# A two-block transformer kernel: the second feed-forward's pairs computed with seven half-size products, and another PSUM bank for one of them

## The chip, the cores and the metric

The kernel runs as one program on one core of a Trainium2 chip. The metric is the device time of one execution in microseconds (us). Before the change the median of three runs is 1746.8 us (1745.65 to 1747.08). The engines are named as in the profile: PE is TensorE (matmuls), PEld its weight loads, DVE VectorE, ACT ScalarE, POOL GpSimd, SP the engine that issues most DMAs.

## The reference

Two transformer blocks run one after the other over 512 tokens with 1024 channels, in float32. Each ends in a gated feed-forward of 2816 hidden channels, and only these two feed-forwards are touched:

```python
D_FF = ((8 * D_MODEL + 3 * 256 - 1) // (3 * 256)) * 256        # 2816
# first block
u = rms_norm(h, norm_ffn_g[l])
g, up = jnp.split(u @ w_gate_up[l], 2, axis=-1)
h = h + (jax.nn.silu(g) * up) @ w_down[l]
# second block
h = rmsnorm(x, g_ffn_pre[l])
gu = h @ w_ffn_in[l]
f = (jax.nn.silu(gu[..., :D_FF_2]) * gu[..., D_FF_2:]) @ w_ffn_out[l]
x = x + rmsnorm(f, g_ffn_post[l])
```

The rest of the first block is a block-sparse attention, a chunked mLSTM and their gated merge; the rest of the second is three attentions and their gated merge.

## The kernel before, in words

**Layout.** Activations lie with channels on the 128 partitions and tokens along the free dimension. Every float32 operand is split into a high part `hi` (a rounding copy on ACT) and a low part `lo` (the difference, on DVE), and each product is three matmuls: hi·hi, hi·lo, lo·hi. All of them are issued through `mm` (L231), so the trace shows one line for nearly all PE work. Weights come from HBM in chunks (`raw`, two buffers) and are split by `emit_split` (L331: ACT at L358, DVE at L359) into `whi` and `wlo`, six buffers each (`NSPLIT`). `next_half` (L364) decides how far ahead of the matmuls the splitting runs; in "deep" mode it fills all six buffers.

**A feed-forward** (`ffn`, L1261) has 22 pairs. A pair is one tile of 128 gate channels and one of 128 up channels. They are done in three parts of 8, 7 and 7 pairs; after each part the down projection adds that part's contribution to all 8 output tiles. A normal pair is 2 tiles x 8 k-tiles x 3 = 48 matmuls of 512 columns (`fm_tile`, L394). Gate and up tiles accumulate in the three PSUM banks `pd`; DVE multiplies them by the row norm `R`, ACT applies silu, DVE multiplies gate and up, and the result is split again into hi and lo (tiles `Ba`/`Bb` and `Ca`/`Cb`).

**Seven products.** `SEVEN = {"f1": 1}` (L131): in the first feed-forward all pairs but the first are computed as a 2 x 2 block product with seven half-size products in place of eight. The blocks are gate/up, the two halves of the 1024 input channels, and the two halves of the 512 tokens. Each product is 4 k-tiles x 3 = 12 matmuls of 256 columns, so a pair has 84 of them. It needs sums of weight blocks and sums of activation blocks. The weight sums `s1` and `s3` are made by accumulating DMAs on the POOL queue (L306, L307: the transfer issued by SP at L304 and L305 is added to), two more on DVE (L322). The activation sums `t1` to `t4` are made once per feed-forward in four steps by `seven_prep` (L412): step k makes four 256-column differences in the tile `M4` (one buffer) on DVE (L428 to L431), a rounding copy of all four on ACT and their lo part on DVE (both through `split_to`, L537 and L538). A product reads k-tile k of them, so the fourth step is needed by the last three matmuls of the first product with a `t`.

`seven` (L438) orders the products of a pair as head ("11"), mid ("t3", "t2", "21", "t1") and tail ("22", "t4"); a pair's tail is issued after the head of the next one. There are three accumulators: `g0` (11, then 21), `g1` (t2, t1, 22, begun from a copy of `g0` made by ACT at L459, "the seeding copy") and `c0` (t3, t4). `g0` and `c0` are the two halves of one `ps` bank; the `g1` of even and odd pairs are the two halves of a bank `po` that is set to zero once (L435). PE runs the products in exactly this order (`strict`, L221).

**The second feed-forward** (`f2`) has no seven products. Its first three pairs are done in two passes over token halves (`fm_halves`, L491), so that the first half of the tokens starts while the second half's norm is still being made: POOL adds up squares (L597), a matmul with ones sums over channels, POOL takes the power -0.5 (L603, `rc_q`), PE broadcasts it by four transposes (L615) and ACT copies it into `R`. The first four of those six half-pass weight blocks, and likewise the first four of the last six down blocks, are split into tiles of their own, tags `Yh`, `Yl`, `Y` and `G` (`self.place`, L255).

The instruction order on each engine is made by the framework's scheduler when the program is built; engines run their queues in that order. Pools give a buffer only after its last reader.

Of the kernel before, what the change touches and what calls it, by code (L numbers as in the profile page):

```python
# [8 lines left out]
F32 = mybir.dt.float32  # L9
F32R = mybir.dt.float32r  # L10
# [7 lines left out]
P = 128  # L18
# [109 lines left out]

SEVEN = {"f1": 1}  # L131
HEAD, MID, TAIL = ("11",), ("3", "2", "12", "1"), ("4", "22")
NWARM = 40
MOBA_C = 0
# [2 lines left out]
NSPLIT = 6  # L137
# [9 lines left out]
class Build:  # L147
# [216 lines left out]
    def next_half(self, expect, ahead=None):  # L364
        i = self.wi
        name, ci, j, L, kt, w = self.halves[i]
        assert name == expect, (name, expect)
        if ahead is None and self.deep:
            cost = lambda k: 0 if k in self.place else 1 if self.halves[k][0].endswith("_7") else CUT
            n, ahead = cost(i), 0  # L370
            while i + ahead + 1 < len(self.halves) and n + cost(i + ahead + 1) <= NSPLIT:
                ahead += 1
                n += cost(i + ahead)
        elif ahead is None:
            ahead = 0 if expect in TOKEN_MAJOR else 1
        while self.next_split <= i + ahead and self.next_split < len(self.halves):
            self.emit_split()
        self.wi += 1
        return self.split.pop(i)
# [32 lines left out]
    def seven_prep(self, u, th, tl, src, g):  # L412


        nc = self.nc
        lo, hi = slice(0, 256), slice(256, 512)
        x = {}
        for i, (d, w) in enumerate(((0, lo), (4, lo), (4, hi))):
            x[("11", "21", "22")[i]] = [lambda k, p=p, d=d, w=w: u[p][:, k + d, w] for p in range(2)]
        for i in range(4):  # L420
            x["t%d" % (i + 1)] = [lambda k, p=p, i=i: p(k)[:, i, :] for p in (th, tl)]

        def step(k):
            a, b = self.tmp(), self.tmp()
            self.act(a, src(k), AF.Copy, scale=g(k))
            self.act(b, src(k + 4), AF.Copy, scale=g(k + 4))
            t = self.t("M4", [P, 4, 256])
            nc.vector.tensor_sub(t[:, 0, :], a[:, lo], a[:, hi])  # L428
            nc.vector.scalar_tensor_tensor(t[:, 1, :], t[:, 0, :], -1.0, b[:, hi], op0=ALU.mult, op1=ALU.subtract)
            nc.vector.tensor_sub(t[:, 2, :], b[:, hi], a[:, hi])  # L430
            nc.vector.scalar_tensor_tensor(t[:, 3, :], t[:, 1, :], -1.0, b[:, lo], op0=ALU.mult, op1=ALU.subtract)  # L431
            self.split_to(th(k), tl(k), t)

        self.seeded = self.bk_o()
        nc.tensor.matmul(self.seeded, self.zb, self.zb[:, None, :].to_broadcast([P, 4, P]), start=True, stop=True)  # L435
        return x, [lambda k=k: step(k) for k in range(4)]

    def seven(self, name, x, pairs, evac):  # L438

        nc = self.nc

        def product(ps, b, start=False):
            hi, lo = x[b]
            kw = dict(skip_group_check=True)
            for k, (wh, wl) in enumerate(self.next_half(name)):
                self.mm(ps, wh, hi(k), start=start and k == 0, stop=False, **kw)
                self.mm(ps, wh, lo(k), start=False, stop=False, **kw)
                self.mm(ps, wl, hi(k), start=False, stop=k == 3, **kw)  # L450

        def head(q):
            b = self.bk_s()
            q["g0"], q["c0"] = b[:, 0:256], b[:, 256:512]
            q["g1"] = self.seeded[:, 256 * (q["j"] % 2):256 * (q["j"] % 2) + 256]
            product(q["g0"], "11", True)

        def mid(q):
            nc.scalar.copy(q["g1"], q["g0"])  # L459
            q["u2"], q["u4"] = self.t("s7", [P, 256], F32, bufs=2), self.t("s7b", [P, 256], F32, bufs=1)  # L460
            product(q["c0"], "t3")
            product(q["g1"], "t2")
            nc.scalar.copy(q["u2"], q["g1"])
            product(q["g0"], "21")
            product(q["g1"], "t1")
            nc.scalar.copy(q["u4"], q["g1"])
            q["lin"] = self.tmp()
            nc.vector.tensor_add(q["lin"][:, 256:512], q["u4"], q["c0"])

        def tail(q):  # L470
            product(q["g1"], "22")
            gate = evac[0](q["g0"], q["g1"])
            product(q["c0"], "t4")
            nc.vector.tensor_add(q["lin"][:, 0:256], q["u2"], q["c0"])
            evac[1](q["j"], gate, q["lin"])
            self.done_tile(lambda: None)

        self.strict = "start"
        last = None
        for j in pairs:  # L480
            q = dict(j=j)
            head(q)
            if last is not None:
                tail(last)
            mid(q)
            last = q
        if last is not None:
            tail(last)
        self.strict = None

    def fm_halves(self, name, n, rhs_hi, rhs_lo, evac, between=None):  # L491
# [766 lines left out]
        yield from self.pipeline(units, [s0, s1, s2, s2b, s3])  # L1258


    def ffn(self, name, u, st, down_evac, part_hook=None, halves=None, x7=None):  # L1261
        nc = self.nc
        uh, ul = u
        rh, rl = self.acc_k(uh), self.acc_k(ul)
        f0 = 0
        for p, n in enumerate(FF_PARTS):
            ah, al = self.pair_tiles("Ba", "Bb"), self.pair_tiles("Ca", "Cb")
            sil = {}

            full = slice(0, S)  # L1270

            def ev_g(ps, j, w=full):
                a = self.tmp()[:, w]
                nc.vector.tensor_mul(a, ps, st["R"][:, w])
                self.last_silu = self.act(a, a, AF.Silu).ins
                sil[j, w.start] = a

            def ev_u(ps, j, w=full):
                b = self.tmp()[:, w]
                nc.vector.tensor_mul(b, ps, st["R"][:, w])  # L1280
                a = sil.pop((j, w.start))
                nc.vector.tensor_mul(a, a, b)
                self.split_to(ah(j)[:, w], al(j)[:, w], a)

            j0 = 0
            if halves is not None and p == 0:
                j0 = NUP // 2
                self.fm_halves(name + "_up", NUP, rh, rl, lambda ps, i, w: (ev_u if i % 2 else ev_g)(ps, i // 2, w),
                               halves)
                self.strict = None  # L1290

            def ev_7g(g0, g1):
                a = self.tmp()
                nc.vector.tensor_mul(a[:, 0:256], g0, st["R"][:, 0:256])
                nc.vector.tensor_mul(a[:, 256:512], g1, st["R"][:, 256:512])
                self.last_silu = self.act(a, a, AF.Silu).ins
                return a

            def ev_7(j, a, lin):
                nc.vector.tensor_mul(lin, lin, st["R"])  # L1300
                nc.vector.scalar_tensor_tensor(a, lin, -1.0, a, op0=ALU.mult, op1=ALU.mult)
                self.split_to(ah(j), al(j), a)

            j7 = n if name not in SEVEN else min(max(SEVEN[name] - f0, j0), n)
            for j in range(j0, j7):
                self.fm(name + "_up", rh, rl, lambda ps, j=j: ev_g(ps, j))
                self.fm(name + "_up", rh, rl, lambda ps, j=j: ev_u(ps, j))
            self.seven(name + "_7", x7, range(j7, n), (ev_7g, ev_7))
            f0 += n
            if part_hook is not None:  # L1310
                part_hook(p)
            k0 = KD - NDN if halves is not None and p == 2 else KD
            for k in range(k0):
                self.fm(name + "_dn", ah, al, lambda ps, k=k: down_evac(ps, k, p, full))
            if k0 < KD:
                self.fm_halves(name + "_dn", NDN, ah, al, lambda ps, i, w: down_evac(ps, k0 + i, p, w))


    def block1(self):
        nc = self.nc  # L1320
        x = self.x
        u = uh, ul = self.new_u()
# [7 lines left out]
        for k in range(KD):  # L1330
            i = k % 2
            self.sq_add(accs[i], x[:, k, :], k < 2, eng=nc.gpsimd if i == 0 else nc.vector)
        st, hooks = self.stat_hooks(accs, "a")
# [17 lines left out]
        q = lambda h: qt_[:, h, :]  # L1351
# [86 lines left out]
        u = uh, ul = self.new_u()  # L1438
        acc = self.t("A", [P, S], F32, bufs=2)

        def ev_wo(ps, k):
# [3 lines left out]

        th = [self.t(tag, [P, 2, 4, 256], F32R) for tag in ("Yh", "Yl")]
        tl = [self.t(tag, [P, 2, 4, 256], F32R) for tag in ("V8", "K8")]
        x7, steps = self.seven_prep(u, lambda k: th[k // 2][:, k % 2], lambda k: tl[k // 2][:, k % 2],
                                    lambda k: h[:, k, :], lambda k: self.vec("norm_ffn_g", k))
        for k in range(KD):  # L1450
            self.fm("wo", *mp["m"], lambda ps, k=k: ev_wo(ps, k))
# [47 lines left out]
    def block2(self, nx):  # L1499
        nc = self.nc  # L1500
# [4 lines left out]
        u = uh, ul = nx["u"]  # L1505
# [231 lines left out]
        def between():  # L1737
            self.hooks = list(hx[256])
# [27 lines left out]
                else:  # L1766
                    self.later = [[0, g] for g in hk + [e[1] for e in self.later] + fs]

        self.ffn("f2", u, st, ev_dn, None, between)

    def run(self):
        self.prologue()
# [80 lines left out]
```

## Time and profile before

| | |
|---|---|
| profiled execution, whole | 1746.25 us |
| its span (first to last instruction) | 1744.3 us |
| median of three runs | 1746.8 us |
| PE busy | 1717.9 us, 98% |
| DVE busy | 1128.6 us, 65% |
| ACT busy | 871.2 us, 50% |
| granted TensorE clock, mean | 0.994 of 2.4 GHz |

Busy times count overlapping instructions once. A matmul's recorded duration is longer than its distance to the next one, since matmuls are pipelined; what a matmul costs is read from start to start. In the rows below a time is the start of an instruction in us from the start of the span, followed by its duration; brackets hold the idle time ahead of it and what ended it.

### The profile page before, as it was taken

The numbers are of one execution on the slowest core, as the hardware profiler recorded it, in microseconds if no ns is written. First come the engines' busy times: TensorE is split into PE (matmuls) and PEld (weight loads), VectorE is DVE, ScalarE is ACT, GpSimd is POOL, SyncE is SP. The second block draws the span as 40 slices with busy tenths as digits, with TensorE's granted clock in tenths as the row PEclk, the third lists the DMA queues.
The fourth block names the chain that finished last, engine by engine and source line by source line (L and its number), as shares of the span: only waits on it lengthen the run. The fifth ranks groups of instructions, "written<-read, shape, count | busy, mean of one in ns | idle before, by whom it ended". The sixth has DMA issues, their size and how long they took to land.

```text
span 1744.3 us, 25883 instructions
## 1 busy us (share of the span) xinstructions
PE 1717.9 (98%) x9601; PEld 1446.7 (83%) x9601; DVE 1128.6 (65%) x2363; ACT 871.2 (50%) x1767; POOL 152.6 (9%) x203
## 2 busy tenths in 40 slices
PE   8999999998999999999999999999999999999997
PEld 8878788887998989988989776777789988888887
DVE  5887665667865857787499945666655743344454
ACT  5755655545543635574455567654545433332331
POOL 1400011000100101000000222200001400000001
PEclk9999999999999999999999999999999999999999
DMA  5433225343654746335224122333233233333331
GB/s 181 119 100 117 78 61 151 121 145 85 163 146 121 179 130 151 83 116 172 85 73 122 49 73 61 109 85 111 71 121 107 63 99 95 97 92 99 95 112 50
DMA packets 65661, 187.04 MB, mean 107 GB/s; under 512 B 7840, under 2 KB 10440, under 8 KB 65280
## 3 DMA queue, kind: packets, MB, share of 16 engines
q1 hardware_dynamic: 59456, 174.33, 32.7%
q0 software_dynamic: 6080, 11.08, 3.9%
q8 instruction: 75, 1.23, 0.3%
q14 instruction: 50, 0.41, 0.1%
HBM read 174.87 MB, written 6.84 MB: 104 GB/s over the span
## 4 chain that ended last, share of the span: by engine, by line
PE 95%; DVE 2%; ACT 2%; POOL 0%; DMA 0%; issue 0%; SPq 0%; DVEq 0%; ACTq 0%
PE pd L231 67%; PE ps L231 7%; PE po L231 5%; PE po L797 2%; PE pd L524 2%; PE pd L526 2%; PE pd L525 2%; PE ps L574 1%; PE ps L575 1%; PE ps L787 1%; PE po L1196 1%; PE ps L1162 0%; DVE ul L541 0%; PE ps L1167 0%; PE po L973 0%
## 5 line engine op out<-in xcount | busy, mean ns | idle before, releaser
L358 ACT CAST whi<-raw 128x512 fp32r<-128x512 f32 (+3 forms) x536 | 308.2, 582 | 498.9 <-PE pd L231 383.7
L359 DVE TENSOR_TENSOR wlo<-raw,whi 128x512 fp32r<-128x512 f32 (+3 forms) x536 | 346.7, 652 | 246.2 <-ACT whi L358 241.4
L231 PE MATMUL pd<-uh,whi 128*128 128x512 f32 (+1 forms) x1032 | 406.0, 394 | 0.0
L231 PE MATMUL pd<-uh,wlo 128*128 128x512 f32 (+1 forms) x1032 | 405.1, 393 | 0.0
L231 PE MATMUL pd<-ul,whi 128*128 128x512 f32 (+1 forms) x1032 | 404.0, 391 | 0.0
L231 PEld LDWEIGHTS pd<-uh,wlo 128*128 128x128 f32 x1032 | 194.0, 188 | 45.4 <-issue 3.3
L231 PEld LDWEIGHTS pd<-ul,whi 128*128 128x128 f32 x1032 | 193.8, 188 | 41.3 <-issue 1.7
L231 PEld LDWEIGHTS pd<-uh,whi 128*128 128x128 f32 x1032 | 194.0, 188 | 40.7 <-issue 2.2
L231 PE MATMUL pd<-Ba,whi 128*128 128x512 f32 (+1 forms) x240 | 91.4, 381 | 0.0
L231 PE MATMUL pd<-Ca,whi 128*128 128x512 f32 (+1 forms) x240 | 90.9, 379 | 0.0
L231 PE MATMUL pd<-Ba,wlo 128*128 128x512 f32 (+1 forms) x240 | 90.7, 378 | 0.0
L231 PE MATMUL pd<-Cb,whi 128*128 128x512 f32 (+1 forms) x210 | 79.7, 380 | 0.0
L231 PE MATMUL pd<-Bb,wlo 128*128 128x512 f32 (+1 forms) x210 | 79.7, 379 | 0.0
L231 PE MATMUL pd<-Bb,whi 128*128 128x512 f32 (+1 forms) x210 | 78.3, 380 | 0.7 <-ACT Bb L537 0.7
L231 PE MATMUL pd<-Yh,whi 128*128 128x512 f32 (+1 forms) x192 | 72.5, 383 | 0.9 <-DVE H L753 0.9
L231 PE MATMUL pd<-Yl,whi 128*128 128x512 f32 (+1 forms) x192 | 72.4, 377 | 0.0
L231 PE MATMUL pd<-Yh,wlo 128*128 128x512 f32 (+1 forms) x192 | 72.4, 377 | 0.0
L526 PE MATMUL pd<-whi,ul 128*128 128x260 f32 (+1 forms) x232 | 64.9, 286 | 1.5 <-DVE ul L541 1.4
L524 PE MATMUL pd<-whi,uh 128*128 128x260 f32 (+1 forms) x232 | 65.4, 286 | 0.8 <-ACT uh L180 0.8
L525 PE MATMUL pd<-wlo,uh 128*128 128x260 f32 (+1 forms) x232 | 65.2, 283 | 0.0
L231 PEld LDWEIGHTS pd<-Ba,whi 128*128 128x128 f32 x240 | 45.0, 188 | 9.7 <-DVE H L1460 0.9
L231 PEld LDWEIGHTS pd<-Ba,wlo 128*128 128x128 f32 x240 | 45.1, 188 | 9.2
(525 smaller groups left out, 3698.4 us busy)
## 6 DMA issues: line engine op xcount, KB each, us to landing
raw<-in_wts SPq DMA_DIRECT2D x218, 512.0 KB, 3.5
raw<-in_wts SPq DMA_DIRECT2D x32, 448.0 KB, 3.4
PT<-in_wts SPq DMA_DIRECT2D x42, 256.0 KB, 3.8
PT<-in_wts POOLq DMA_DIRECT2D x42, 256.0 KB, 5.0
P<-in_wts SPq DMA_DIRECT2D x21, 256.0 KB, 3.2
raw<-in_wts SPq DMA_DIRECT2D x8, 520.0 KB, 3.5
tabd<-tab SPq DMA_DIRECT2D x8, 320.0 KB, 5.7
H<-in_xT SPq DMA_DIRECT2D x8, 256.0 KB, 5.1
```

Source lines behind the costliest of these rows:

```text
L231: return self.pe(self.nc.tensor.matmul(*args, **kw))
L358: self.nc.scalar.copy(hi, r)
L359: self.nc.vector.tensor_sub(lo, r, hi.bitcast(F32))
L524: mm(pss[i][:, :w], xh[:, kk, sl], hi, start=(kk == 0), stop=False)
L525: mm(pss[i][:, :w], xh[:, kk, sl], lo, start=False, stop=False)
L526: mm(pss[i][:, :w], xl[:, kk, sl], hi, start=False, stop=(kk == 7))
L574: mm(out, q, khi, start=True, stop=False)
L575: mm(out, q, klo, start=False, stop=True)
L787: nc.tensor.transpose(ps[:, kt * P:(kt + 1) * P], Pt[:, kt * P:(kt + 1) * P], self.ident)
L797: nc.tensor.matmul(o[64 * hh:64 * hh + 64, qt * P:(qt + 1) * P], v[:, kt, h * 64:(h + 1) * 64], PTs[hh][:, kt * P:(kt + 1) * P], start=(kt ...
L1196: nc.tensor.matmul(o[c][64 * hh:64 * hh + 64, kt * P:], bv[:, kt, h * 64:(h + 1) * 64], us[hh]["a"][:, :N], start=False, stop=True, skip_g ...
```

## The change

1. `SEVEN = {"f1": 2, "f2": 5}`: in the first feed-forward the second pair becomes a normal pair, so 20 pairs in place of 21 are done with seven products; in the second feed-forward pairs 5 to 21, 17 of 22, are.
2. `c0` gets a bank of its own (one of the three `pd` banks) in place of the second half of `g0`'s bank, and the seeding copy is issued behind the previous pair's product "22", ahead of its "t4".
3. In the second feed-forward the sums `t1` to `t4` are made by `halves_done`, called when the two passes are issued; the four steps are issued behind the first and second tile of pair 3. Their hi parts lie in `Yh` and `Yl`, their lo parts in the tags `Y` and `G`. Deep mode is switched on there.
4. In deep mode the splitting no longer runs ahead into a block that has a place of its own, so the four last down blocks are split into `Yh`, `Yl`, `Y` and `G` only when the products that read the sums there have been issued.

```diff
-SEVEN = {"f1": 1}
+SEVEN = {"f1": 2, "f2": 5}
...
-            while i + ahead + 1 < len(self.halves) and n + cost(i + ahead + 1) <= NSPLIT:
+            while i + ahead + 1 < len(self.halves) and n + cost(i + ahead + 1) <= NSPLIT and \
+                    i + ahead + 1 not in self.place:
...
-            self.split_to(th(k), tl(k), t)
+            nc.scalar.copy(th(k)[0], t)
+            n = 4 // len(tl(k))
+            for i, d in enumerate(tl(k)):
+                w = slice(i * n, (i + 1) * n)
+                nc.vector.tensor_sub(d, t[:, w, :], th(k)[0][:, w, :].bitcast(F32))
...
         def head(q):
-            b = self.bk_s()
-            q["g0"], q["c0"] = b[:, 0:256], b[:, 256:512]
+            q["g0"], q["c0"] = self.bk_s()[:, 0:256], self.bk_d()[:, 0:256]
...
+        def seed(q):
+            nc.scalar.copy(q["g1"], q["g0"])
+
         def mid(q):
-            nc.scalar.copy(q["g1"], q["g0"])
...
-            product(q["c0"], "t3")
+            product(q["c0"], "t3", True)
...
-        def tail(q):
+        def tail(q, between):
             product(q["g1"], "22")
+            between()
             gate = evac[0](q["g0"], q["g1"])
...
-            if last is not None:
-                tail(last)
+            if last is None:
+                seed(q)
+            else:
+                tail(last, lambda: seed(q))
             mid(q)
...
+        def halves_done():
+            th = [self.t(tag, [P, 2, 4, 256], F32R) for tag in ("Yh", "Yl")]
+            tl = [self.quad(tag, F32R, [P, 2, 256]) for tag in ("Y", "G")]
+            x7, steps = self.seven_prep(u, lambda k: [th[k // 2][:, k % 2]], lambda k: tl[k // 2][2 * (k % 2):2 * (k % 2) + 2],
+                                        X, lambda k: self.vec("g_ffn_pre_2", k))
+            self.later += [[1 + k // 2, f] for k, f in enumerate(steps)]
+            self.deep = True
+            return x7
```

**ACT, first feed-forward, one pair's change to the next.** Before, the seeding copy (L459, `po<-ps`) stands behind the silu of the previous pair (L180):

```order
L466 COPY s7b_5156<-po_4055 128x256
L358 CAST whi_5246<-PT_4845 128x512
L358 CAST whi_5268<-raw_5131 128x512
L180 ACTIVATE tmp_5262<-tmp_5262 128x512
L459 COPY po_4055<-ps_5229 128x256
L358 CAST whi_5292<-T_5294 128x512
```

Now (L465) it stands ahead of that silu and of one more weight cast:

```order
L473 COPY s7b_4747<-po_4055 128x256
L358 CAST whi_4908<-PT_4551 128x512
L358 CAST whi_4939<-raw_4793 128x512
L465 COPY po_4055<-ps_4888 128x256
L358 CAST whi_4960<-T_4962 128x512
```

The copy has moved up by one ACT instruction, and on PE the product behind it ("t3") writes another bank.

**DVE, second feed-forward, behind the up tile of the fifth pair (pair 4).** `pd` is that tile; `M` is `M4`, `G` the lo part of the sums, `Yl` their hi part. Before:

```order
L1280 TENSOR_TENSOR tmp_15175<-pd_15150,R_13970 128x512
L359 TENSOR_TENSOR wlo_15225<-raw_15180,whi_15224 128x512
L1282 TENSOR_TENSOR tmp_15137<-tmp_15137,tmp_15175 128x512
L538 TENSOR_TENSOR Cb_14522<-tmp_15137,Bb_14520 128x512
L359 TENSOR_TENSOR wlo_15261<-raw_15218,whi_15260 128x512
```

Now:

```order
L1290 TENSOR_TENSOR tmp_15224<-pd_15199,R_13925 128x512
L1292 TENSOR_TENSOR tmp_15186<-tmp_15186,tmp_15224 128x512
L359 TENSOR_TENSOR wlo_15240<-raw_15151,whi_15239 128x512
L438 TENSOR_TENSOR G_14985<-M_3267_15123,Yl_14980 128x512
L438 TENSOR_TENSOR G_14986<-M_3267_15123,Yl_14980 128x512
L359 TENSOR_TENSOR wlo_15257<-T_15258,whi_15256 128x512
L548 TENSOR_TENSOR Cb_14477<-tmp_15186,Bb_14475 128x512
L430 TENSOR_TENSOR M_3270_15135<-tmp_15131 128x256
L432 TENSOR_TENSOR M_3270_15135<-tmp_15132,tmp_15131 128x256
L322 TENSOR_TENSOR T_15394<-T_15309,raw_15151 128x512
L431 SCALAR_TENSOR_TENSOR M_3270_15135<-M_3270_15135,tmp_15132 128x256
L433 SCALAR_TENSOR_TENSOR M_3270_15135<-M_3270_15135,tmp_15132 128x256
```

The lo part of the third step and the whole fourth step stand behind the evacuation of pair 4's up tile; the ACT cast of the fourth step and two more `L438` follow.

**POOL, second feed-forward, the end of the second token half's sum of squares.** `A` is the sum, `PT_15002` and the like the weight sums of pairs 5 and 6. Before:

```order
L597 TENSOR_TENSOR A_13969<-A_13969,PT_14664 128x256
L597 TENSOR_TENSOR A_13969<-A_13969,PT_14672 128x256
L597 TENSOR_TENSOR A_13969<-A_13969,PT_14680 128x256
L603 TENSOR_TENSOR rc_q_14859<-small_14857,mhalf_142 128x2
L603 TENSOR_TENSOR rc_z_17341<-small_17339,mhalf_142 128x2
```

Now:

```order
L607 TENSOR_TENSOR A_13924<-A_13924,PT_14627 128x256
L306 DMA PT_15002<-in_wts 128x512
L607 TENSOR_TENSOR A_13924<-A_13924,PT_14635 128x256
L307 DMA PT_15001<-in_wts 128x512
L306 DMA PT_15072<-in_wts 128x512
L307 DMA PT_15071<-in_wts 128x512
L613 TENSOR_TENSOR rc_q_14814<-small_14812,mhalf_142 128x2
```

Four accumulating DMAs have come ahead of `rc_q`, one of them ahead of the last addition. Each waits until the transfer that it adds to has landed, and that transfer until its buffer is free of the sums of squares.

## Rows read from the trace of the kernel before

**Rows 1.** The page: busy time by engine; shares of the chain that ended last.
```profile
PE 1717.9 (98%) x9601; PEld 1446.7 (83%) x9601; DVE 1128.6 (65%) x2363; ACT 871.2 (50%) x1767; POOL 152.6 (9%) x203
...
PE 95%; DVE 2%; ACT 2%; POOL 0%; DMA 0%; issue 0%; SPq 0%; DVEq 0%; ACTq 0%
```
**Rows 2.** Windows: five seven-product pairs (first feed-forward), three normal pairs (second).
```profile
core 0: us, PE busy (x) PEld busy (x) DVE busy (x) ACT busy (x) POOL busy (x), PEclk, DMA share, GB/s
444.76:495.87 51.11, 50.95 (x423) 49.93 (x421) 45.69 (x80) 31.64 (x61) 7.81 (x9) 1.00 0.74 184
...
1415.03:1448.39 33.36, 33.36 (x145) 27.03 (x144) 15.69 (x25) 11.22 (x19) 0.00 (x0) 1.00 0.30 95
```
**Rows 3.** Timeline of PE at one seeding copy: start, duration, line, operation.
```profile
465.24 0.28 PE L231 MATMUL ps<-K,whi 128*128 128x256 f32 x1
465.36 0.28 PE L231 MATMUL ps<-Yl,wlo 128*128 128x256 f32 x1
465.67 0.38 PE L231 MATMUL ps<-Yh,whi 128*128 128x256 f32 x1
465.89 0.28 PE L231 MATMUL ps<-V,whi 128*128 128x256 f32 x1
```
**Rows 4.** Waits of PEld for the seeding copy: us in total, times, longest.
```profile
PEld ps L231 <- ACT po L459: 7.5, 21, 1.1
```
**Rows 5.** Timeline of PE at the second part's first seven-product pair.
```profile
550.92 0.29 PE L231 MATMUL ps<-uh,wlo 128*128 128x256 f32 x1
552.06 0.39 PE L231 MATMUL ps<-Yh,whi 128*128 128x256 f32 x1 [0.86 <-ACT po L459]
```
**Rows 6.** Timeline of PE in the first feed-forward's first seven-product pair.
```profile
432.34 0.49 PE L231 MATMUL ps<-Yl,whi 128*128 128x256 f32 x1 [3.69 <-ACT Yl L537]
433.60 0.58 PE L231 MATMUL ps<-K,whi 128*128 128x256 f32 x1 [0.77 <-DVE K L538]
433.98 0.41 PE L231 MATMUL ps<-Yl,wlo 128*128 128x256 f32 x1
```
**Rows 7.** Windows behind that wait.
```profile
433.98:439.31 5.33, 5.33 (x27) 5.33 (x26) 1.39 (x2) 1.51 (x3) 0.00 (x0) 0.50 0.19 52
```
**Rows 8.** Timeline of DVE around the same wait.
```profile
426.45 0.68 DVE L1280 TENSOR_TENSOR tmp<-pd,R 128x512 f32<-128x512 f32 x1
427.04 0.41 DVE L428 TENSOR_TENSOR M<-tmp 128x256 f32<-128x256 f32 x1
427.38 0.42 DVE L430 TENSOR_TENSOR M<-tmp,tmp 128x256 f32<-128x256 f32 x1
...
432.32 1.23 DVE L538 TENSOR_TENSOR K<-M,Yl 128x1024 fp32r<-128x1024 f32 x1 [0.51 <-ACT Yl L537]
```
**Rows 9.** Timeline of ACT there: the fourth step's cast.
```profile
431.24 1.05 ACT L537 CAST Yl<-M 128x1024 fp32r<-128x1024 f32 x1 [0.66 <-DVE M L431]
```
**Rows 10.** Timeline of POOL at the second feed-forward's second norm.
```profile
1376.06 5.31 POOL L597 TENSOR_TENSOR A<-A,PT 128x256 f32<-128x256 f32 x6
1384.63 0.71 POOL L603 TENSOR_TENSOR rc_q<-small,mhalf 128x2 f32<-128x2 f32 x1 [3.26 <-DVE small L631]
```
**Rows 11.** Timeline of PE there: the sum over channels, the broadcast.
```profile
1382.78 0.50 PE L231 MATMUL ps<-ones,A 128*128 128x1 f32 x4
...
1386.05 0.38 PE L615 MATMUL ps<-cst,rc_q 128*128 128x128 f32 x2
```
**Rows 12.** DMA issues: size of one, median us from issue to landing.
```profile
PT<-in_wts SPq DMA_DIRECT2D x42, 256.0 KB, 3.8
```
**Rows 13.** Timeline of POOL in the first feed-forward: an accumulating DMA.
```profile
458.53 0.86 POOL L306 DMA_DIRECT2D PT<-in_wts  x1 [2.93 <-DVE T L322]
```
**Rows 14.** Groups by line and shape: busy, mean ns of one.
```profile
L358 ACT CAST whi<-raw 128x512 fp32r<-128x512 f32 x412 | 252.3, 620 | 379.0 <-PE pd L231 267.5 <-DMA raw<-in_wts 53.4 <-PE po L231 35.1
```
**Rows 15.** Timeline of PE in the second feed-forward's first pass: the last of four short waits.
```profile
1360.36 0.38 PE L231 MATMUL pd<-ul,Yh 128*128 128x256 f32 x1 [0.72 <-DVE ul L541]
```
**Rows 16.** Windows shortly behind these waits.
```profile
1363.45:1367.84 4.39, 4.39 (x23) 4.39 (x22) 1.44 (x3) 1.93 (x4) 0.70 (x1) 0.51 0.65 166
```

More of the change, by code (lines that the diff above doesn't have):

```diff
@@ L420, in seven_prep @@
         for i in range(4):
-            x["t%d" % (i + 1)] = [lambda k, p=p, i=i: p(k)[:, i, :] for p in (th, tl)]
+            x["t%d" % (i + 1)] = [lambda k, p=p, i=i: p(k)[i * len(p(k)) // 4][:, i % (4 // len(p(k))), :]
+                                  for p in (th, tl)]
         def step(k):
@@ L452, in head @@
         def head(q):
-            b = self.bk_s()
-            q["g0"], q["c0"] = b[:, 0:256], b[:, 256:512]
+            q["g0"], q["c0"] = self.bk_s()[:, 0:256], self.bk_d()[:, 0:256]
             q["g1"] = self.seeded[:, 256 * (q["j"] % 2):256 * (q["j"] % 2) + 256]
+            q["u2"], q["u4"] = self.t("s7", [P, 256], F32, bufs=2), self.t("s7b", [P, 256], F32, bufs=1)
             product(q["g0"], "11", True)
+        def seed(q):
+            nc.scalar.copy(q["g1"], q["g0"])
         def mid(q):
-            nc.scalar.copy(q["g1"], q["g0"])
-            q["u2"], q["u4"] = self.t("s7", [P, 256], F32, bufs=2), self.t("s7b", [P, 256], F32, bufs=1)
-            product(q["c0"], "t3")
+            product(q["c0"], "t3", True)
             product(q["g1"], "t2")
@@ L487, in seven @@
         if last is not None:
-            tail(last)
+            tail(last, lambda: None)
         self.strict = None
@@ L1258, in memattn, with ffn @@
         yield from self.pipeline(units, [s0, s1, s2, s2b, s3])
-    def ffn(self, name, u, st, down_evac, part_hook=None, halves=None, x7=None):
+    def ffn(self, name, u, st, down_evac, part_hook=None, halves=None, x7=None, halves_done=None):
         nc = self.nc
@@ L1290, in ffn @@
                 self.strict = None
+                x7 = halves_done()
             def ev_7g(g0, g1):
@@ L1447, in block1 @@
         tl = [self.t(tag, [P, 2, 4, 256], F32R) for tag in ("V8", "K8")]
-        x7, steps = self.seven_prep(u, lambda k: th[k // 2][:, k % 2], lambda k: tl[k // 2][:, k % 2],
+        x7, steps = self.seven_prep(u, lambda k: [th[k // 2][:, k % 2]], lambda k: [tl[k // 2][:, k % 2]],
                                     lambda k: h[:, k, :], lambda k: self.vec("norm_ffn_g", k))
@@ L1767, in ev_dn @@
                     self.later = [[0, g] for g in hk + [e[1] for e in self.later] + fs]
-        self.ffn("f2", u, st, ev_dn, None, between)
+        def halves_done():
[6 more added lines that the diff above has]
+            return x7
+        self.ffn("f2", u, st, ev_dn, None, between, None, halves_done)
     def run(self):
```

## The prediction

> **What bounds the kernel now.** I read the page first: PE is busy for 98% of the span and holds 95% of the chain that ended last [rows 1]. So the time is PE's instruction stream plus the places where it stands still, and a change pays by fewer PE cycles or by a pause that goes. Next I compared the two forms of a pair in windows between equal instructions, both at a granted clock of 1.00 (2.4 GHz). Five seven-product pairs took 51.11 us, 10.22 each; three normal pairs 33.36 us, 11.12 each, or 0.2317 us for each of 48 matmuls [rows 2]. DVE was busy 45.69 us in the first window, 9.14 us a pair or 89%, and 47% in the second: seven products load DVE nearly as much as PE.
>
> Then I looked inside a seven-product pair for pauses. Its matmuls start 0.12 us apart, except where the seeding copy stands: 0.31 and then 0.22 [rows 3], a loss of 0.29 us. PEld waits for that copy 21 times, once a pair [rows 4]. Without it a pair is 10.22 - 0.28 = 9.95 us (rounded; 84 x 0.1184). In a part's first pair nothing lies between the head and the copy: the gap is 1.14 us in place of 0.12 [rows 5], a loss of 1.02 and 0.1 behind it. The largest pause is in the very first such pair: PE waits 3.69 us for the hi part of the fourth step and 0.77 us for its lo part [rows 6]. Against the usual spacing the gaps are 3.84, 1.14 and 0.26 us too long, 5.24 together. Behind it PE runs 5.33 us at a granted 0.50, the 1.2 GHz level, with 25 matmuls 0.213 us apart [rows 7]: 25 x 0.095 = 2.4 us more.
>
> **The change part by part, first feed-forward.**
> - The bank: 18 copies inside a part at 0.29 are 5.3 us, three at a part's start at 1.13 are 3.4 us. The copy now runs while "22" to "t3" are on PE (36 matmuls, 4.3 us), of which it needs 0.37. That is its cover. Gain 8.7; at the least 0, if another wait stands there at once.
> - One pair becomes normal: 11.12 - 9.95 = 1.2 us more.
> - The first seven-product pair comes 11 us later, and the four steps stand on DVE ahead of the evacuation of pair 0 now. The pause and its slow stretch go: 5.2 + 2.4 = 7.6. What is late next is that evacuation itself: pair 1's up tile needs the bank that pair 0's gate tile leaves, and I charge 0.3 us for it (0 to 1.5).
> Sum: -8.7 + 1.2 - 7.6 + 0.3 = -14.8 us.
>
> **Second feed-forward, the pairs.** 17 x (11.12 - 9.95) = -19.9 us. At one place a page of the Trainium skill speaks against this. The rows give 0.1184 us for a matmul of half width and 0.2317 for a full one; seven products win as long as the first is under 0.2317 x 48/84 = 0.1324 [rows 2]. "TensorE: Matmul & The Clock Gate", section "Back-to-back issue gap", says that in a stream of weight loads and matmuls the small ones pay more for each column, and gives 81 ns for 128 columns and 131 ns for 512. A straight line between these gives an estimate of 98 ns for 256, so a pair would go from 48 x 131 = 6.3 to 84 x 98 = 8.2 us, and 16 more such pairs would cost some 30 us. Both forms stand in this trace at sustained full clock, and they contradict it. I keep the rows.
>
> **Second feed-forward, the beginning.** This is the largest cost. Let U be the end of pair 4's up tile on PE. DVE can't evacuate it earlier, and its queue holds the fourth step behind that. Rows give 0.60 us from start to start for 512 columns, 0.34 for 256 [rows 8], and 1.05 for the step's cast [rows 9]. From U + 0.2: seven instructions of 512 columns to 4.4, two of 256 to 5.1, one of 512 to 5.7, two of 256 to 6.4, the cast to 7.6, two subtractions (1.23 as one [rows 8]) to 9.0. PE needs the hi part after "11" (1.42) and nine matmuls (1.07), at U + 2.5. It gets it at 7.6 and the lo part at 9.0, so "t3" ends near U + 9.2 in place of 2.8: 6.4 us. The same wait cost 5.24 in the first feed-forward, the nearest row. The fall to 1.2 GHz should follow as it did there: 2.5 us. Ends: 0, were DVE and ACT ahead of PE enough, and 11.
>
> **The norm behind the POOL queue.** `rc_q` starts at 1384.63 and PE needs it at 1386.05 [rows 10, 11]. Now four accumulating DMAs precede it, 0.86 us each [rows 13], one ahead of the last of the additions, which end at 1381.4 [rows 10]. The transfers that they add to can be issued as the `PT` buffers come free, one each 0.9 us from about 1378 to 1380.5, and land 3.8 us later [rows 12]: 1381.6 to 1384.4. Then POOL has the last addition done at 1383.2, the fourth DMA issued near 1385.5, `rc_q` at 1386.3. PE waits 0.4 at the channel sum (1382.78) and some tenths at the broadcast. I take 1.0 us; 0 at the least, 5 if the transfers queue behind the five `P` transfers ahead of them.
>
> **The last down blocks.** `Yh` is free only when the last "t4" has read its sums. Let E be the end of that product. The cast of the first block ends at E + 0.4, its lo part at 1.25; PE has one full-width matmul left and waits 0.8. Then it runs 18 half-width ones (2.1 us) to E + 3.2 and needs pair 21's result, which stands on DVE behind six subtractions and products (3.4 us from E + 0.55) and an ACT cast of 0.62 [rows 14]: 4.65, so 1.5 more, and 0.2 for its lo part. That is 2.5 us. Four short waits of 2.1 us together in the first pass (the last of them [rows 15]) were followed by 4.39 us at 0.51 [rows 16], 2.2 us lost; I take half of that, 1.2. Ends: 0 and 5. The handing over to the down projection at the end of parts 0 and 1 I put at 0.4 together, as the small gaps in the first feed-forward show.
>
> Sum of the second feed-forward: -19.9 + 6.4 + 2.5 + 1.0 + 2.5 + 1.2 + 0.4 = -5.9 us. In all -20.7 us from the profiled execution's own 1746.25 us: 1725.6. The median shown is 0.55 us above that execution, so I predict **1726 us**.
>
> **Rivals.**
> - *The steps are ready in time.* The four steps begin some 20 us ahead of U. If DVE had U's evacuation late or the fourth step early, the 8.9 us go: 1717. Against it stands the order itself, in which the step is behind U. Chance 0.12.
> - *POOL's queue decides.* If the five `P` and four `PT` transfers come one behind the other, `rc_q` is some 5 us late, PE stops at the broadcast, and the fall to 1.2 GHz adds 2.4: 1726 + 6.4 = 1732. For it: nine transfers of 256 KB in some 9 us. Chance 0.17.
> - *The bank wait only changes its name.* DVE at 9.14 of 9.95 us is 92% of a pair. If `wlo` or the gate's evacuation come late, a pair stays near 10.2: 37 x 0.28 = 10.4 us back, 1736. This is also the case in which the new bank does not do what it says. Chance 0.10.
> - *DVE sets the pace*, the slower side. A pair has 12 DVE instructions of 512 columns (0.69 alone) and 4 of 256 (0.42): 9.96 us if none overlaps, more than PE's 9.95, with each wait for ACT on top. The trace has them overlap, 0.60 from start to start. Lost are all 20.7 us once 37 pairs take 0.56 us more, 10.5 each; at 10.7 the time is 1726 + 37 x 0.75 = 1754. Five pairs at 10.22 with PE unstopped elsewhere speak against it. With half-width matmuls getting dearer, 0.05.
>
> **How the numbers follow.** The forecast holds 0.56; its own range from the bounds is 1721 to 1731. The range of 8 in 10 reaches from the first rival's value to the third's, 1717 to 1736; half of each of these lies beyond, and the fourth: 0.06 + 0.05 + 0.05 = 0.16. What a measurement of this kernel can tell from no change is about 0.2%, 3.5 us. Faster by more: 0.56 + 0.12 + 0.17 + 0.10 less 0.01 for a worse tail = 0.94; within 0.02; slower 0.04.
>
> **What would show it.** In the profile after: no wait of `ps` or `pd` matmuls for the seeding copy, and seven-product pairs 9.95 us apart in both feed-forwards; no gap of several us in the first feed-forward's first such pair; one of some 4 us for `Yl` and 1.3 us for `G` at the second's, then a stretch at 0.50; at most 1 us of PE waiting at `rc_q`; 2 to 3 us of short waits at the last down blocks. Pairs over 10.1 us, or a PE wait of over 2 us at L615, would make the prediction wrong.

## The result and the profile after

Four runs each: 1726.84 us (1726.3 to 1727.66) against 1746.61 us (1745.65 to 1747.08), a ratio of 0.9888 with a 95% interval of 0.9871 to 0.9905; the two ranges do not overlap. The forecast was 1726. The profiled execution took 1726.64 us, its span is 1724.9 us.

A span can be cut at instructions that both programs have (FF is the feed-forward). The cuts are starts on PE: the channel sum that stands ahead of the first feed-forward (`ps<-ones,A` at 421 us), the first down tile of its last part (`pd<-Ba,whi`, 512 columns), the first half-width matmul of the second feed-forward (`pd<-uh,Yh`), its first normal pair, and the end.

| us | start to first FF | first FF | between | first passes and norm | rest of second FF |
|---|---|---|---|---|---|
| before | 421.01 | 308.44 | 625.77 | 42.20 | 346.88 |
| after | 420.62 | 294.61 | 625.90 | 43.80 | 339.97 |
| difference | -0.39 | -13.83 | +0.13 | +1.60 | -6.91 |
| forecast | 0 | -14.8 | 0 | +1.0 | -6.9 |

The first cut does not divide the same work in both programs. The windows up to it, before and after (the columns are those of [rows 2]), hold 2218 and 2215 matmuls:

```profile
0.00:421.01 421.01, 416.40 (x2218) 343.08 (x2219) 285.99 (x712) 244.91 (x520) 40.15 (x49) 1.00 0.38 117
```
```profile
0.00:420.62 420.62, 416.26 (x2215) 342.87 (x2216) 284.97 (x710) 244.53 (x519) 39.16 (x48) 1.00 0.38 118
```

Three matmuls of 512 columns, 0.7 us, have moved behind the channel sum. For the same work the first feed-forward is 14.5 us shorter and the stretch ahead of it 0.3 us longer. The same holds for every run below that starts the first feed-forward's seven products at pair 2.

**The pairs.** The window over five seven-product pairs of the second feed-forward, in the same columns:

```profile
1504.16:1553.81 49.65, 49.65 (x423) 49.65 (x422) 44.21 (x80) 31.09 (x60) 8.66 (x10) 1.00 0.77 184
```

That is 9.93 us a pair, against 10.22 and 11.12 in [rows 2], at the same granted clock. DVE is busy 89% and PE never stops. Between "t4" and "t3", where [rows 3] has its 0.31 us, the matmuls now start 0.12 us apart:

```profile
447.41 0.28 PE L231 MATMUL pd<-K,whi 128*128 128x256 f32 x1
447.53 0.28 PE L231 MATMUL pd<-Yl,wlo 128*128 128x256 f32 x1
447.65 0.28 PE L231 MATMUL pd<-Yh,whi 128*128 128x256 f32 x1
447.77 0.28 PE L231 MATMUL pd<-V,whi 128*128 128x256 f32 x1
```

**The start of the second feed-forward's products.** PE, the first such pair; it answers to [rows 6]:

```profile
1410.73 0.39 PE L231 MATMUL pd<-G,whi 128*128 128x256 f32 x1 [1.14 <-DVE G L438]
...
1415.08 0.58 PE L231 MATMUL pd<-Yl,whi 128*128 128x256 f32 x1 [3.85 <-ACT Yl L434]
1416.40 0.58 PE L231 MATMUL pd<-G,whi 128*128 128x256 f32 x1 [0.75 <-DVE G L438]
1416.78 0.41 PE L231 MATMUL pd<-Yl,wlo 128*128 128x256 f32 x1
```

Start to start the four gaps are 1.30, 4.01, 1.20 and 0.26 us too long, 6.8 together. On DVE and ACT, the evacuation of pair 4's up tile and the fourth step's cast and lo part:

```profile
1407.38 0.69 DVE L1290 TENSOR_TENSOR tmp<-pd,R 128x512 f32<-128x512 f32 x1 [0.73 <-PE pd L231]
...
1415.05 1.29 DVE L438 TENSOR_TENSOR G<-M,Yl 128x512 fp32r<-128x512 f32 x2 [1.11 <-ACT Yl L434]
```
```profile
1413.98 1.04 ACT L434 CAST Yl<-M 128x1024 fp32r<-128x1024 f32 x1 [3.86 <-DVE M L433]
```

With U at 1407.2 the hi part is there at U + 7.8 and the lo part at U + 9.1; the forecast had 7.6 and 9.0. Windows around the wait:

```profile
1412.00:1413.00 1.00, 0.00 (x0) 0.00 (x0) 1.00 (x3) 0.00 (x0) 0.00 (x0) 0.83 0.90 160
1413.00:1414.00 1.00, 0.00 (x0) 0.00 (x0) 0.91 (x3) 0.02 (x1) 0.00 (x0) 0.50 0.09 14
...
1416.78:1419.53 2.75, 2.75 (x14) 2.75 (x14) 0.69 (x1) 0.62 (x1) 0.00 (x0) 0.51 0.04 13
```

The clock falls to 1.2 GHz while PE stands, and only 2.75 us of work are left to run at it, in place of the 5.33 of [rows 7].

**The norm.** POOL, which answers to [rows 10], and PE, to [rows 11]:

```profile
1361.96 4.44 POOL L607 TENSOR_TENSOR A<-A,PT 128x256 f32<-128x256 f32 x5
1368.18 0.92 POOL L306 DMA_DIRECT2D PT<-in_wts  x1 [1.78 <-ACT tmp L180]
1368.83 1.04 POOL L607 TENSOR_TENSOR A<-A,PT 128x256 f32<-128x256 f32 x1
1369.50 1.23 POOL L307 DMA_DIRECT2D PT<-in_wts  x1
1370.08 1.55 POOL L306 DMA_DIRECT2D PT<-in_wts  x1
1370.62 1.91 POOL L307 DMA_DIRECT2D PT<-in_wts  x1
1371.21 2.06 POOL L613 TENSOR_TENSOR rc_q<-small,mhalf 128x2 f32<-128x2 f32 x1
```
```profile
1369.92 0.61 PE L231 MATMUL ps<-ones,A 128*128 128x1 f32 x4 [1.00 <-POOL A L607]
...
1373.33 0.43 PE L625 MATMUL ps<-cst,rc_q 128*128 128x128 f32 x2
```

Six additions in a row have become five, a pause of 1.78 us, a DMA issue and the sixth. PE waits for that sixth one and not at the broadcast. For the pause the profile names an ACT instruction; the transfer that this DMA adds to was issued at 1363.79 and by the median of [rows 12] landed near 1367.6, so which of the two came last is not told apart here.

**The last down blocks, and a handing over.** PE and its weight loads at the end of the second feed-forward, and PE at the end of the first one's second part:

```profile
1677.69 0.36 PE L231 MATMUL pd<-Ba,Yh 128*128 128x256 f32 x1 [0.38 <-DVE tmp L482]
...
1681.59 0.50 PE L231 MATMUL pd<-Bb,whi 128*128 128x512 f32 x1 [1.24 <-ACT Bb L547]
...
1684.69 0.38 PE L231 MATMUL pd<-Ba,Yl 128*128 128x256 f32 x1 [0.94 <-DVE H L1764]
```
```profile
1677.66 0.19 PEld L231 LDWEIGHTS pd<-Ba,Yh 128*128 128x128 f32 x1 [0.67 <-ACT Yh L358]
```
```profile
619.09 0.50 PE L231 MATMUL pd<-Ba,whi 128*128 128x512 f32 x1 [0.51 <-DVE tmp L482]
```

The end has 3.7 us of gaps at a clock of 1.00. At the first of them the weight load waits for the cast of `Yh`. The last row was not in the forecast: a down tile waits for the addition that reads `c0` (L482).

### The profile page after: what moved, and what is told of

The parts are those of the page before. It is cut to its first block, busy times and chain, and to the rows that moved or that the text cites. A ratio compares the mean times of both kernels' runs of the same rounds, so it can differ in the third digit from the quotient of the medians.

```text
span 1724.9 us, 27517 instructions
## 1 busy us (share of the span) xinstructions
PE 1696.0 (98%) x10178; PEld 1459.9 (85%) x10178; DVE 1197.8 (69%) x2515; ACT 916.4 (53%) x1875; POOL 180.1 (10%) x235
## 5 line engine op out<-in xcount | busy, mean ns | idle before, releaser
L358 ACT CAST whi<-raw 128x512 fp32r<-128x512 f32 (+2 forms) x504 | 288.3, 580 | 410.2 <-PE pd L231 269.3
L359 DVE TENSOR_TENSOR wlo<-raw,whi 128x512 fp32r<-128x512 f32 (+2 forms) x504 | 324.9, 650 | 204.8 <-ACT whi L358 198.8
L231 PE MATMUL pd<-uh,whi 128*128 128x512 f32 (+1 forms) x776 | 305.1, 393 | 0.0
L231 PE MATMUL pd<-uh,wlo 128*128 128x512 f32 (+1 forms) x776 | 304.5, 392 | 0.0
L231 PE MATMUL pd<-ul,whi 128*128 128x512 f32 (+1 forms) x776 | 303.5, 391 | 0.0
L231 PE MATMUL pd<-Yl,whi 128*128 128x256 f32 (+1 forms) x340 | 114.3, 336 | 3.8 <-ACT Yl L434 3.8
L231 PE MATMUL pd<-Yh,whi 128*128 128x256 f32 (+1 forms) x340 | 114.3, 339 | 0.9 <-DVE H L763 0.9
L231 PE MATMUL pd<-Yh,wlo 128*128 128x256 f32 (+1 forms) x340 | 114.0, 335 | 0.0
L231 PE MATMUL ps<-ul,whi 128*128 128x256 f32 x296 | 83.2, 281 | 0.0
L231 PE MATMUL ps<-uh,wlo 128*128 128x256 f32 x296 | 83.1, 281 | 0.0
```

What stands on the lines that cost most here:

```text
L231: return self.pe(self.nc.tensor.matmul(*args, **kw))
L358: self.nc.scalar.copy(hi, r)
L359: self.nc.vector.tensor_sub(lo, r, hi.bitcast(F32))
```

## The experiments

All were measured beside the kernel before, whose medians in these comparisons were 1746.3 to 1747.3 us. The medians are of four to nine executions; the stretches are those of the table above, each from one profiled execution, and the stretch ahead of the first feed-forward is left out:

| us | median | first FF | between | norm | rest |
|---|---|---|---|---|---|
| bank and early copy, first FF | 1742.09 | 300.58 | 627.18 | 42.22 | 347.90 |
| early copy alone | 1741.27 | 301.80 | 625.77 | 42.78 | 346.78 |
| bank alone | 1740.32 | 300.60 | 626.54 | 42.14 | 346.98 |
| all of the first FF | 1733.41 | 294.64 | 625.72 | 42.27 | 347.28 |
| second FF from pair 6 | 1721.11 | 294.60 | 625.93 | 43.60 | 333.38 |
| four steps at once | 1728.00 | 294.60 | 625.93 | 45.43 | 340.84 |
| sums behind `rc_q` | 1725.86 | 294.60 | 625.93 | 42.46 | 340.29 |
| last pair normal | 1725.94 | 294.66 | 625.91 | 43.43 | 338.19 |
| second FF from pair 15 | 1729.83 | 294.64 | 625.93 | 44.14 | 342.61 |
| pair 6, last pair normal | 1717.81 | 294.66 | 625.92 | 43.43 | 330.45 |
| the three edits | 1716.49 | 294.60 | 625.96 | 42.16 | 330.48 |

### The first feed-forward taken apart

Bank and early copy alone (this run and the three that follow also make no sums in the second feed-forward):

```diff
-SEVEN = {"f1": 2, "f2": 5}
+SEVEN = {"f1": 1}
...
-                x7 = halves_done()
+                x7 = halves_done() if name in SEVEN else None
```

> Only the own bank and the early seeding copy: the first feed-forward starts its seven products at pair 1 as before, the second has none. My theory: 18 copies x 0.28 and three at 1.13 us go, 8.5 to 8.7 us less, so about 1738; pairs 9.95 us apart; the 5.2 us pause in the first such pair and its stretch at 0.50 stay. Rival, the wait only changes its name: pairs stay near 10.2 us and the time is within 2 us of 1746.6.

The early copy alone, on top of that:

```diff
-            q["g0"], q["c0"] = self.bk_s()[:, 0:256], self.bk_d()[:, 0:256]
+            b = self.bk_s()
+            q["g0"], q["c0"] = b[:, 0:256], b[:, 256:512]
...
-            product(q["c0"], "t3", True)
+            product(q["c0"], "t3")
```

> As the run above, but c0 is again the second half of g0's bank; only the place of the copy is changed. Theory A, time of the copy decides: inside a part the copy is done before t3, so 18 x 0.28 us go, and the three gaps of 1.13 us at a part's start stay: about 1741.5. Theory B, the shared bank decides, whenever the copy runs: t3 still waits once a pair, 1746. Theory C, as A but the copy also covers the parts' starts: 1738.

The bank alone, again on top of the first of these edits:

```diff
-            if last is None:
-                seed(q)
-            else:
-                tail(last, lambda: seed(q))
+            if last is not None:
+                tail(last, lambda: None)
+            seed(q)
             mid(q)
```

> The other half alone: c0 in its own bank, the copy behind the previous pair's tail as before. The 12 matmuls of t3 (1.42 us) now lie between the head and the first user of the copy, which needs 0.37 us. Theory A (cover is enough): pairs 9.95 us, about 1738, the same as with both. Theory B (the copy stands in ACT's queue behind casts that wait for PE): t2 waits for it, some 0.1 to 0.3 us a pair, 1740 to 1746.

The whole change in the first feed-forward alone:

```diff
-SEVEN = {"f1": 2, "f2": 5}
+SEVEN = {"f1": 2}
```

> The whole change in the first feed-forward (from pair 2, own bank, early copy), none in the second. My theory: the terms of the two feed-forwards add, so this shows the first one's alone, 13.8 us less: about 1733; against the run with pair 1, 1.2 us for a normal pair and some 6 to 7.6 us less for the pause. Rival: part of the difference between the two traces comes from elsewhere (another layout of the program), then it is 1729 or 1737.

In the first feed-forward the bank alone does what both do: 300.60 and 300.58 us, 7.85 less than before. The windows over four pairs of the second part show it, first the bank alone, then the early copy alone:

```profile
562.03:601.75 39.72, 39.72 (x338) 39.72 (x337) 37.06 (x65) 24.90 (x49) 6.94 (x8) 1.00 0.75 186
```
```profile
558.67:598.40 39.73, 39.73 (x338) 39.73 (x337) 36.17 (x65) 24.90 (x48) 6.30 (x8) 1.00 0.74 185
```

Inside a part either is enough, 9.93 us a pair. At a part's start only the bank helps; with the early copy alone the gap of [rows 5] stands unchanged:

```profile
548.75 0.39 PE L231 MATMUL ps<-Yh,whi 128*128 128x256 f32 x1 [0.86 <-ACT po L466]
```

So by the traces theory A held for both halves. The bank's 8.7 us came out 0.8 smaller here, by three things. In the very first pair the copy's wait is gone, but the pause for the fourth step behind it is 4.98 us too long in place of 3.84, which takes 1.1 back. Behind that pause PE has some 3 us of work at half clock in place of 5.33, which gives 1.0. And 0.8 us are lost at the handing over, with the bank and not without it: the next `pd` bank that the down projection asks for is the one that held `c0`. Here it is with the bank alone; with the shared bank no down tile waits there:

```profile
626.36 0.50 PE L231 MATMUL pd<-Ba,whi 128*128 128x512 f32 x1 [0.51 <-DVE tmp L482]
```

Starting at pair 2 takes another 5.94 us (300.58 to 294.64), or 6.6 for the same work; 6.1 were forecast (7.6 less 1.2 less 0.3).

In the medians the expectations of the first and the third run missed: 1742.1 and 1740.3 against 1738. The third even lies where its theory B had it, but in its window PE is busy for all of 39.72 us, so no wait of `t2` is the reason. The second hit 1741.5 (1741.3), although its first feed-forward gained 6.6 us and not the 5 that this asks for. In the profiled execution of the first run 0.8 us of some 4 are missing in the first feed-forward itself; the others stand where this edit changes nothing that is computed: ahead of it (+0.8), "between" (+1.4) and "rest" (+1.0). Ahead of it the clock is at half for a while in this run and not in the kernel before, with PE busy in both (first this run, then before):

```profile
22.00:24.00 2.00, 2.00 (x11) 2.00 (x11) 0.14 (x2) 0.00 (x0) 1.04 (x1) 0.50 0.74 268
```
```profile
22.00:24.00 2.00, 2.00 (x18) 2.00 (x19) 0.88 (x3) 0.00 (x0) 1.04 (x1) 1.00 0.68 152
```

What made the other two stretches longer stays open.

### The beginning of the second feed-forward

```diff
-SEVEN = {"f1": 2, "f2": 5}
+SEVEN = {"f1": 2, "f2": 6}
```

> The changed kernel, but the second feed-forward starts its seven products at pair 6 in place of 5. My theory: the waits for Yl and G and the stretch at 0.50 are the price of pair 5 coming too early, because the fourth step ends 9.1 us behind pair 4's up tile; with a normal pair 5 (11.1 us) between they go. 6.9 + 1.2 us less, 1.2 more for the normal pair: about 1720. Rival: DVE has no room for the steps there; the wait only moves to pair 5's banks or to pair 6, and the time is 1726 to 1728.

```diff
-            self.later += [[1 + k // 2, f] for k, f in enumerate(steps)]
+            self.later += [[1, f] for f in steps]
```

> The changed kernel with all four steps issued behind the first tile of pair 3 in place of two behind the first and two behind the second. On DVE two of the fourth step's four differences now stand ahead of pair 4's up tile, and pair 3's up tile is evacuated later. Theory A (queue position is the cause): the fourth step is ready 1.5 to 3 us earlier, 1723.5 to 1725.5. Theory B (DVE is simply full from 1393 to 1413, 90% busy): nothing is gained, 1726 to 1728.

From pair 6 the waits and the slow stretch are gone. The fourth step's cast on ACT ends at 1416.39, and PE first reads `Yl` at 1419.74:

```profile
1415.34 1.05 ACT L434 CAST Yl<-M 128x1024 fp32r<-128x1024 f32 x1
```
```profile
1419.74 0.28 PE L231 MATMUL pd<-Yl,whi 128*128 128x256 f32 x1
```

The rest is 6.59 us shorter; 6.9 were forecast. With the four steps issued at once, DVE has part of the fourth step ahead of the up tile's evacuation (`L1290`):

```profile
1411.29 0.42 DVE L430 TENSOR_TENSOR M<-tmp 128x256 f32<-128x256 f32 x1
1411.63 0.42 DVE L432 TENSOR_TENSOR M<-tmp,tmp 128x256 f32<-128x256 f32 x1
1411.96 0.69 DVE L359 TENSOR_TENSOR wlo<-T,whi 128x512 fp32r<-128x512 f32 x1
1412.57 0.68 DVE L1290 TENSOR_TENSOR tmp<-pd,R 128x512 f32<-128x512 f32 x1
...
1414.70 0.42 DVE L433 SCALAR_TENSOR_TENSOR M<-M,tmp 128x256 f32<-128x256 f32 x1
```

and PE has its hi part 30.18 us behind the first normal pair, against 30.15 in the changed kernel (1416.44 - 1386.26 and 1415.08 - 1384.93). The third step's wait is gone, the fourth's is longer, the sum 6.9 against 6.8. The up tile's evacuation comes 26.31 us behind the first normal pair in place of 22.45. In the 20 us behind 1393 DVE of the changed kernel is busy 18.29:

```profile
1393.00:1413.00 20.00, 17.09 (x83) 13.96 (x82) 18.29 (x36) 12.45 (x20) 1.75 (x2) 0.99 0.41 106
```

By the waits theory B held: what is drawn forward on DVE pushes something else back. The median, 1728.0, is no proof of it: this run's norm is 1.6 us longer, and from 1372 to 1375 us its granted clock is 0.50 with PE busy, where the changed kernel has 1.00. Nothing shows that the edit caused this.

### The norm and the last pair

```diff
...
+        with ExitStack() as order:
+            if self.chunks[ci][0] > self.f2_off:
+                order.enter_context(self.tc.issue_after(self.last_pow))
-        nc.gpsimd.dma_start(s3, src[:, 0:L], accum_op=ALU.add)
-        nc.gpsimd.dma_start(s1, src[:, 0:L], accum_op=ALU.add)
+            nc.gpsimd.dma_start(s3, src[:, 0:L], accum_op=ALU.add)
+            nc.gpsimd.dma_start(s1, src[:, 0:L], accum_op=ALU.add)
...
```

(`last_pow` is the power on POOL that makes `rc_q`, `f2_off` the place of the second feed-forward's normal pairs in the weights.)

> The changed kernel, but the accumulating DMAs of the second feed-forward's weight sums are ordered behind rc_q on POOL. My theory: the wait at the sum over channels (1.16 us) and 0.4 us around it go, 1.6 us less: about 1725.2, and the stretch from the first half pass to the first normal pair is 42.2 us again. Rival: the sums are then late for pair 5, or the stretch at half clock behind the first pass is what made it longer: no change.

```diff
-            self.seven(name + "_7", x7, range(j7, n), (ev_7g, ev_7))
+            e7 = n - 1 if name == "f2" and p == 2 else n
+            self.seven(name + "_7", x7, range(j7, e7), (ev_7g, ev_7))
+            for j in range(e7, n):
+                self.fm(name + "_up", rh, rl, lambda ps, j=j: ev_g(ps, j))
+                self.fm(name + "_up", rh, rl, lambda ps, j=j: ev_u(ps, j))
...
```

(The part left out lays down pair 21's weights as a normal pair needs them.)

> The changed kernel, but pair 21 of the second feed-forward is a normal pair, so that the sums in Yh, Yl, Y and G are read for the last time a pair earlier. My theory: the waits at the last down blocks (3.7 us) come from the sums' tiles being free too late and from the longer way to a seven-product pair's result; they fall to about 0.3 us as before the change, at 1.2 us for the normal pair: 2.2 us less, about 1724.6. Rival: the waits come from DVE being behind in general: then 1.2 us more, 1728.

With the DMAs behind `rc_q` the six additions run in a row again and the channel sum does not wait:

```profile
1361.57 5.32 POOL L612 TENSOR_TENSOR A<-A,PT 128x256 f32<-128x256 f32 x6
1370.15 0.71 POOL L618 TENSOR_TENSOR rc_q<-small,mhalf 128x2 f32<-128x2 f32 x1 [3.26 <-DVE small L646]
1370.81 0.91 POOL L311 DMA_DIRECT2D PT<-in_wts  x1
```

The norm takes 42.46 us in place of 43.80. With a normal last pair no matmul waits in the last down blocks, and the rest is 1.78 us shorter: the 3.7 us of gaps less 1.2 for the pair would be 2.5, so 0.7 comes back behind them. Of this 0.6 stands in the closing norm: from its channel sum (`ps<-ones,tmp`, 1714.32 and 1711.02) to the end it is 10.6 us in the changed kernel and 11.2 here; why is open. My theory had two reasons, the sums' tiles free too late and the longer way to pair 21's result; this run takes both away and does not tell them apart.

### The price of a pair, and the three together

```diff
-SEVEN = {"f1": 2, "f2": 5}
+SEVEN = {"f1": 2, "f2": 15}
```

> The changed kernel, but the second feed-forward has seven products only in its last part (pairs 15 to 21). Against the run that starts at pair 6, nine pairs more are normal. My theory (9.95 against 11.12 us a pair): 9 x 1.17 = 10.5 us more, less 0.7 for one handing over to the down projection: about 1731. Rival, narrow matmuls pay more for each column in such a stream (the Trainium skill, TensorE: Matmul & The Clock Gate, section Back-to-back issue gap: by the estimate from it a seven-product pair costs 1.9 us more than a normal one): 17 us less, 1704.

Nine pairs fewer than from pair 6 cost 9.23 us in the rest (342.61 - 333.38). By 11.12 - 9.93 they would cost 10.7, less 0.8 and 0.3 for the two handings over that go: 9.6. Narrow matmuls are not dearer here than the rows of before said. The rival with the estimate from the Trainium skill ("TensorE: Matmul & The Clock Gate", section "Back-to-back issue gap") fails by its sign: it had a gain of 17 us.

> Three edits together: seven products in the second feed-forward from pair 6, the accumulating DMAs behind rc_q, pair 21 normal. If the three terms add, as measured in their own stretches: 7.1 + 0.8 + 2.6 = 10.5 us less than the changed kernel, about 1716. Rival: they share slack (the place of the sums and the start at pair 6 both relieve DVE and POOL in the same 20 us): 1718 to 1720.

Here the POOL order reached only the sums behind pair 21, so this run joins two edits: 9.52 us less in the rest, the norm at 43.43, as long as with the normal last pair alone. Alone the two gave 6.59 and 1.78 us, 8.37 together. Of the 1.15 us more, 0.75 are the closing norm, which is 10.8 and 11.2 us long in these two runs and 10.6 here as in the changed kernel; the rest is open. With the order for all of them:

> The three edits again, this time with all accumulating DMAs of the second feed-forward behind rc_q (in the last combination the order bound only those behind pair 21, so its norm stretch stayed 43.4 us). My theory: that stretch falls by 1.2 to 1.4 us as it did with this edit alone, to 42.2 to 42.5 us, and the whole to about 1716.5. Rival: the sums for pair 6 come later and make its first product wait: 1718.

The norm takes 42.16 us and no matmul between it and the closing norm waits over 0.7 us. At 1716.49 us (1715.2 to 1716.9, five runs) it is the fastest version of these, 0.9826 of the kernel before (0.9813 to 0.984); the changed kernel is at 0.9888.

## Why the prediction was right

**The bound.** PE's stream plus its pauses: the differences of the first table are PE matmuls that went, PE gaps that came or went, and work at half clock, but for some 0.5 us in the rest that I did not follow.

**First feed-forward, -14.8 forecast, -13.8 measured, -14.5 for the same work.** The copy's waits and the pause with its slow stretch went, as forecast. Part 0 came out at -8.64, or -9.3 with the three matmuls that moved, where its share of the terms is -8.97; part 1 at -2.90 where it is -2.87; and part 2, with the down projection of part 1, at -2.30 in place of -2.87. That last one holds the handing over at the end of part 1, 0.8 us, which I had put at nothing here. The 0.3 us that I charged for pair 0's evacuation are not in the trace: no matmul of part 0 starts over 0.15 us late. The cover that I named, the 36 matmuls from "22" to "t3", is not what is needed: the 12 of "t3" in another bank are enough.

**The pairs, -19.9.** At 9.93 it is 17 x 1.19 = -20.2; in the run from pair 15 nine pairs cost 9.2 us where this price gives 9.6.

**The beginning, 6.4 + 2.5.** The wait was 6.8 and each of its times within 0.2 us. The clock's part was mis-sized: taken as in [rows 7], it was 2.75 us at half clock, some 1.2 lost. The reason I gave, the fourth step's place behind U in DVE's queue, is not the cause by itself, since moving half of the step ahead of U gained nothing. What the runs show is a DVE queue that is full for 20 us, and a wait that goes when the date moves by one pair.

**The norm, 1.0.** 1.60, of which the experiment gives 1.34 back. The place was the DMA ahead of the last addition, as forecast, with 1.16 at the sum in place of 0.4; the broadcast did not wait.

**The last down blocks, 2.5 + 1.2, and the handings over, 0.4.** The wait for the cast of `Yh` (0.9 us with its lo part) and that for pair 21's result (1.6) came as forecast. The 1.2 for a slow clock did not come; in its place stands a wait that I had not seen, of the same 1.2 us, for the additions that empty the down banks (`H`, L1764). So the 3.7 us are right by luck. The handings over took 1.1 in place of 0.4. As measured, the terms of the rest are -20.2 + 6.8 + 1.2 + 3.7 + 1.1 = -7.4, against -6.91; 0.2 of the difference is a longer closing norm. That -6.9 was forecast and -6.91 measured is luck too: the errors of the terms cancel.

**The rivals.** The steps were not ready. POOL's queue cost 1.2 us at the sum, not 6. The bank's wait did change its name, but at a handing over (0.8 us at the end of the second part of each feed-forward, 0.3 at the end of the second one's first), not once in a pair. DVE at 89% did not set the pace of the pairs.

## What to carry to other kernels

Price a change in the stretch where it acts, between instructions that both programs have: edits worth 7 to 8 us there showed 4 to 6 in the medians, and stretches that no edit touched differed by 1 to 2, in part by falls of the clock. Count the work on both sides of a cut: here three matmuls had crossed one. Before an accumulator is put into another ring of banks, look who asks for that ring next. Where new work on a side engine must be ready by a date, count how busy that engine is in the stretch before: here reordering a full queue gained nothing, and moving the date by one pair did.

## What the runs showed of the hardware that I had not expected

The same kind of wait costs different amounts of clock. In the kernel before, the clock was still 0.73 in the microsecond in which PE resumed (432 to 433), and 5.33 us of work ran at half clock behind it. With the early copy alone the pause and the products are the same, but the clock is at 0.50 a microsecond before PE resumes at 432.10 and back sooner (windows of that run):

```profile
431.00:432.00 1.00, 0.00 (x0) 0.00 (x0) 0.57 (x1) 1.00 (x1) 0.00 (x0) 0.50 0.01 0
...
436.00:437.00 1.00, 1.00 (x9) 1.00 (x8) 0.00 (x0) 0.46 (x1) 0.00 (x0) 0.86 0.45 117
```

Its first part gained 3.08 us where six copies at 0.29 explain some 1.75; the other 1.3 us are less work at half clock (2.5 us behind the last wait in place of 5.33). What fixes the moment of the fall stays open here.

The stretch between the two feed-forwards, with the same computation in all kernels, took 625.7 to 627.2 us, and the one ahead of the first 419.9 to 422.0. The kernel alone does not fix this: four executions of one program, the second feed-forward from pair 6, took 1719.1 and 1719.3 us at a mean granted clock of 0.997, and 1722.9 and 1723.2 at 0.995.
